# First mixer: tile 1 for TensorE's convolution is projected ahead of k, v and q and convolved between the first scores; one projected unit stands between attention blocks

## The chip, the cores and the metric

The kernel runs on one core of a Trainium2 chip. The metric is the device time of one execution in microseconds (us): the median of three runs. The engines are called PE (TensorE), DVE (VectorE), ACT (ScalarE), POOL (GpSimd) and SP (SyncE, which issues DMA transfers). L160 is line 160 of the kernel.

## The reference

One inference step of a two-layer decoder: 512 prompt tokens and 8 x 8 sample tokens, 576 columns in all, width 1024, float32. Layer 0 mixes with a gated causal convolution (width 31) beside windowed attention, layer 1 with a Mamba-2 scan; a convolutional feed-forward block follows each. Only the mixer of layer 0 is touched:

```python
def even_mixer(h, conv_hist, k_hist, v_hist, start, w_in, conv_w, conv_b, ln_g, ln_b, qn_g, kn_g, sinks, w_out):
    a_val, a_gate, q, k, v = jnp.split(
        h @ w_in, [CONV_A_DIM, 2 * CONV_A_DIM, 2 * CONV_A_DIM + qd, 2 * CONV_A_DIM + qd + kd], axis=-1)
    u = a_val * jax.nn.sigmoid(a_gate)
    padded = jnp.concatenate([conv_hist, u], axis=1)
    c = jax.nn.silu(layernorm(causal_dwconv(padded, conv_w, conv_b), ln_g, ln_b))
    new_conv = padded[:, -(CONV_A_WIDTH - 1):]
    q = partial_rope(rmsnorm(q.reshape(b, t, N_Q_HEADS, HEAD_DIM), qn_g), pos)
    k = partial_rope(rmsnorm(k.reshape(b, t, N_KV_HEADS, HEAD_DIM), kn_g), pos)
    ...
    out = jnp.concatenate([c, o], axis=-1) @ w_out
    return out, new_conv, k_all[:, -WINDOW:], v_all[:, -WINDOW:]
```

CONV_A_DIM is 512, so the convolution has four tiles of 128 channels. The attention has 8 query heads of 64 on 2 key heads, a window of 128, and a learned sink per head; the prompt is done in four blocks of 128 queries, which see 128 keys (block 0) or 256.

## The kernel before

Channels lie on the 128 partitions, the 576 tokens along them, in two halves of 288. A **unit** (`units`) projects 128 output channels: one weight tile of 128 x 1024 comes by DMA on SP's queue (L141, three buffers `wr`), is split into a high part on ACT (L150) and a low part on DVE (L151), and each half takes 24 matmuls, three for each of eight input tiles (`mm3`, L160 to L162), into a PSUM bank of the ring "mm". Behind each half its closure evacuates the bank: `a_gate(i)` scales and applies the sigmoid, `a_val(i)` writes the gated values of convolution tile i into `cap[i]` and `cas`, and others serve k, v and q (norm sums, rotary product L461, transposes of v). The first mixer has 14 units: gate(i) and val(i) for i = 0 to 3, k, v, q0 to q3.

Tiles 0 and 2 are convolved on DVE with 31 taps each (L434, L436). The taps are handed out a few at a time behind the halves of units (`then_taps`) or alone (`some_taps`). Tiles 1 and 3 (`PC`) are convolved on TensorE by `pe_conv(i)`: the closure of val(i) stores the tile to a scratch in DRAM, `cad[i]` (L415, L416); `pe_conv` builds the weights `w4` on POOL (L544), reads the tile back with 32 transfers on SP's queue, 16 into `xp4` and 16 into `xs4`, each shifted by a column (L555, L556), and then runs 32 matmuls with 32 output columns over the 512 prompt tokens (L563), 32 over the samples (L570), and two evacuations (L574, L575). It is a generator: the first `next` issues weights and transfers, the rest comes when it is taken up again.

Attention per block n: `scores(n)` does eight matmuls (L629) and the softmax, which is DVE's maximum (L601), ACT's exponential (L608), DVE's sums and reciprocals (L609, L610) and POOL's normalisation, one product per head (L612). `values(n)` transposes the probabilities in chunks of 128 keys (L644, TensorE), has ACT copy them out of PSUM (`ptb`, L646), multiplies by v (`po`, L649) and has ACT copy the result (`of`, L657). `sample_loads`, `sample_scores` and `sample_values` do the same for the sample tokens against cached keys. After them the output projection runs over the attention tiles (`oh`), then the layer norm over the four convolved tiles (mean matmul `pm`, L756), then the output projection over these (`cc`).

PSUM has eight banks in rings by purpose; from the first scores on they are mm = [0, 1], aux = [4 to 7], sc = [4, 5, 6], pt = [7, 2], po = [3]. The order of the instructions on each engine is fixed when the program is built: a scheduler takes the program's order as a priority and moves an instruction ahead where another isn't ready, so units, scores and convolution interleave. Each engine then runs its list in that order.

Of the kernel before, what the change touches and what calls it, by code (L numbers as in the profile page):

```python
# [50 lines left out]
class Builder:  # L51
# [300 lines left out]
    def mix0(self):  # L352
# [15 lines left out]
        cos, sin = self.S("cos"), self.S("sin")  # L368
# [21 lines left out]
        PC, NPTB = (1, 3), 3  # L390
# [49 lines left out]
        def some_taps(n):  # L440
            for _ in range(n):
                next(taps, None)

        def then_taps(unit, n):
            src_, m, evac = unit

            def go(half, p):
                evac(half, p)
                some_taps(n)
            return src_, m, go  # L450
# [82 lines left out]
        nc.sync.dma_start(sin, d["sin"])  # L533
        nc.vector.tensor_scalar(pq, self.cv("prot", 0, P), self.pv("q_g"), None, op0=MUL)
        nc.vector.tensor_scalar(pk, self.cv("prot", 0, P), self.pv("k_g"), None, op0=MUL)
        self.units([then_taps(u, n) for u, n in zip(qkv, (1, 2, 1, 1, 1, 1))], 1)
        self.free(kg, ksq, krs, vf, cos, sin)

        self.rings = {"mm": [0, 1], "aux": [4, 5, 6, 7], "sc": [4, 5, 6], "pt": [7, 2], "po": [3]}

        def pe_conv(i):
            w4 = [self.S("w4", NP) for _ in range(2)]
            for a in range(2):
                nc.gpsimd.tensor_tensor(w4[a].rearrange("p (k m) -> p k m", m=32),  # L544
                                        self.cv("m32", 0, 32).unsqueeze(1).broadcast_to([P, 16, 32]),
                                        self.pv("ca_wq", i * 32 + a * 16, 16).unsqueeze(2).broadcast_to([P, 16, 32]), op=MUL)
            xp4 = [self.S("xp4", 540) for _ in range(4)]
            xsp = [self.S("xs4", 608) for _ in range(2)]
            xs4 = [xsp[c // 2][:, (c % 2) * 304:(c % 2) * 304 + 304] for c in range(4)]
            src = cad[i]  # L550
            for c in range(4):
                for j in range(4):
                    n = 540 if j < 3 else 536
                    r, rc = slice(j * 32, j * 32 + 32), slice(c * 32, c * 32 + 32)
                    nc.sync.dma_start(xp4[c][r, 0:n], src[rc, j:j + n])  # L555
                    nc.sync.dma_start(xs4[c][r, 0:304 - j], src[rc, 542 + j:846])  # L556
            yield
            pp, ps = self.pm(), self.pm()
            for s in range(8):
                k = slice(0, P if s < 7 else 96)  # L560
                for c in (3, 2, 1, 0):
                    w = w4[s // 4][k, (s % 4 * 4 + c) * 32:(s % 4 * 4 + c) * 32 + 32]
                    m = nc.tensor.matmul(pp[c * 32:c * 32 + 32, :], w, xp4[c][k, 4 * s:4 * s + NP], start=s == 0, stop=s == 7)  # L563
                    if s or c < 3:
                        self.tc.keep_in_program_order(m)
            for s in range(8):
                k = slice(0, P if s < 7 else 96)
                for c in range(4):
                    w = w4[s // 4][k, (s % 4 * 4 + c) * 32:(s % 4 * 4 + c) * 32 + 32]
                    m = nc.tensor.matmul(bt(ps[c * 32:c * 32 + 32, 0:64]), w, xs4[c].rearrange("p (b t) -> p b t", t=38)[k, :, 4 * s:4 * s + 8],  # L570
                                         start=s == 0, stop=s == 7)
                    self.tc.keep_in_program_order(m)
            ca[i] = self.S("ca")
            nc.vector.tensor_scalar(ca[i][:, :NP], pp, self.pv("ca_b", i), None, op0=ADD)  # L574
            nc.vector.tensor_scalar(ca[i][:, NP:], ps[:, 0:64], self.pv("ca_b", i), None, op0=ADD)  # L575
            self.free(xp4, xsp, w4)
            yield


        rq = self.ps("rq")  # L580
        for bh in range(2):
# [36 lines left out]
        def scores(n):  # L618

            k0 = max(n - 1, 0) * P  # L620
            width = (n + 1) * P - k0
            sc = [None] * 8
            for j in range(4):
                if j % 2 == 0:
                    p = [self.ps("sc", "sc") for _ in range(2)]
                for kv in range(2):
                    rows = slice(kv * 64, kv * 64 + 64)
                    o = sc[kv * 4 + j] = p[kv][:, (j % 2) * width:(j % 2 + 1) * width]
                    nc.tensor.matmul(o, qf[j][rows, n * P:(n + 1) * P], kf[rows, k0:k0 + width], start=True, stop=True)  # L629
            return softmax(sc, self.cv("amask", 256 - width, width), rsq[:, n * 8:n * 8 + 8],  # L630
                           self.pv("sink_p", 0, 8), nsink[:, 0:8], width, (0, 1, 4, 5, 2, 3, 6, 7))

        def values(n, probs):

            pr, held = probs
            po = self.ps("po", "po")
            k0 = max(n - 1, 0)
            nch = n + 1 - k0
            for c in range(nch):
                ptb = []  # L640
                for kv in range(2):
                    pt = self.ps("pt", "pt")
                    for j in range(4):
                        nc.tensor.transpose(pt[:, j * P:(j + 1) * P], pr[kv * 4 + j][:, c * P:(c + 1) * P], self.ident)  # L644
                    ptb.append(self.Z("ptb", NP, bufs=NPTB))
                    nc.scalar.activation(ptb[-1], pt, AF.Copy)  # L646
                ch = k0 + c
                for kv in (1, 0):
                    m = nc.tensor.matmul(po[kv * 64:kv * 64 + 64, :], vt[:, ch * P + kv * 64:ch * P + kv * 64 + 64], ptb[kv],  # L649
                                         start=c == 0, stop=c == nch - 1)  # L650
                    if kv == 0:
                        self.tc.keep_in_program_order(m)
            self.free(held)
            if not of:
                of.extend(self.S("of") for _ in range(4))
            for j in range(4):
                nc.scalar.activation(of[j][:, n * P:(n + 1) * P], po[:, j * P:(j + 1) * P], AF.Copy)  # L657
# [4 lines left out]
        def sample_loads():  # L662
            for i in range(2):
                kct.append(self.S("kct", 512))
                vc.append(self.S("vc", 512))
                nc.sync.dma_start(kct[i], d["kct"][i])
                nc.sync.dma_start(vc[i], d["vc"][i])
                nc.sync.dma_start(d["wk_old"][i], kct[i].rearrange("p (b s) -> p b s", s=P)[:, :, 8:])
                nc.sync.dma_start(d["wv_old"][i], vc[i][8:, :])
# [3 lines left out]
        def sample_scores():  # L673
            for bh in range(2):
                p = [self.ps("sc", "sc") for _ in range(2)]
                for b4 in range(4):
                    b = bh * 4 + b4
                    for kv in range(2):
                        rows = slice(kv * 64, kv * 64 + 64)
                        nc.tensor.matmul(p[kv][b4 * 32:b4 * 32 + 32, 0:P], qs[rows, b * 32:b * 32 + 32],  # L680
                                         kct[bh][rows, b4 * P:(b4 + 1) * P], start=True, stop=True)
                for kv in range(2):
                    rows = slice(kv * 64, kv * 64 + 64)
                    nc.tensor.matmul(p[kv][:, P:192], qs[rows, bh * P:(bh + 1) * P], kf[rows, NP:], start=True, stop=True)
                c0 = 32 + bh * 2
                probs.append(softmax([p[kv][:, 0:192] for kv in range(2)], self.cv("smask", bh * 192, 192), rsq[:, c0:c0 + 2],
                                     self.pv("sink_s", 0, 2), nsink[:, 8:10], 192, (0, 1)))
# [25 lines left out]
                nc.scalar.activation(bt(of[j][:, NP:]), po_v[:, :, j, :], AF.Copy)  # L713

        p0 = scores(0)
        self.units([then_taps(gate_unit(2), 2)], 1)
        p1 = scores(1)
        self.units([then_taps(val_unit(2), 2), then_taps(gate_unit(1), 2)], 1)
        values(0, p0)
        p2 = scores(2)  # L720
        self.units([then_taps(val_unit(1), 2), then_taps(gate_unit(3), 2)], 1)
        values(1, p1)
        p3 = scores(3)
        self.units([then_taps(val_unit(3), 2)], 1)
        self.norm_end()
        convs = [pe_conv(i) for i in PC]
        next(convs[0])
        sample_loads()
        values(2, p2)
        sample_scores()  # L730
        some_taps(5)
        next(convs[1])
        values(3, p3)
        for _ in convs[0]:
            pass
        some_taps(5)
        sample_values()
        for _ in convs[1]:
            pass
        self.rings = {"mm": [2, 3, 0, 1], "aux": [4, 5, 6, 7]}  # L740
        oh = [self.pair("o") for _ in range(4)]
# [608 lines left out]
```

## Time and profile before

| What | us |
|---|---|
| median of three runs | 1605.51 |
| lowest and highest run | 1602.03, 1608.3 |
| profiled execution, its own time | 1610.28 |
| span of its profile | 1608.5 |
| TensorE busy in the span | 1569.8 |
| unit k begins on TensorE | 24.78 |
| last matmuls of the unit q3 end | 73.30 |
| output projection begins | 178.16 |
| convolution of tile 3 begins | 188.17 |

The span is what the profiler saw of one execution; its time is measured around it and is 1.8 us longer. The mean granted clock of TensorE was 0.988 of full speed. Times in the trace count from the span's start. The whole change lies between 24.78 and about 200 us, an eighth of the span; the rest is the other layer and the feed-forward blocks. A row of the timeline gives start, length, engine, line, what is written from what, and in brackets the idle time ahead with what ended it. A group's row gives count, busy time, mean of one in ns, and idle time ahead.

### The profile page before, as it was taken

How to read it: one execution, taken by the hardware profiler on the slowest of the kernel's cores; microseconds unless marked ns; L12 is line 12 of the kernel's file. 1: busy time of each engine (PE TensorE's matmuls, PEld its weight loads, DVE VectorE, ACT ScalarE, POOL GpSimd, SP SyncE). 2: the span in 40 equal slices, each digit the busy share in tenths (PEclk: the TensorE clock that was granted, in tenths of full speed). 3: DMA queues.
4: the chain of work that ended last, by engine and by line, in shares of the span. 5: the costliest groups of instructions: out<-in, count | busy, mean ns of one | idle time of the engine just before them, and what ended most of it. 6: DMA issues, size and time to landing. Idle time of an engine off the chain costs nothing.

```text
span 1608.5 us, 28729 instructions
## 1 busy us (share of the span) xinstructions
PE 1569.8 (98%) x11709; PEld 1484.2 (92%) x11709; DVE 999.5 (62%) x1750; ACT 660.6 (41%) x1213; POOL 150.5 (9%) x362
## 2 busy tenths in 40 slices
PE   8997999999999999999999999999999999999999
PEld 7985699999999999998988998898799999999999
DVE  7877386664455355668786676676776653564552
ACT  6265263222222123479665546556453221221220
POOL 0045001000000000011201101111101000000000
PEclk9998999999999999999999999999999999999999
DMA  7116222222222222226235226236322222222222
GB/s 228 58 57 141 70 79 91 92 79 79 90 81 73 93 83 78 74 82 178 101 87 186 99 74 193 80 104 175 106 80 87 84 80 86 86 71 89 91 82 75
DMA packets 69841, 157.60 MB, mean 98 GB/s; under 512 B 20158, under 2 KB 24510, under 8 KB 69710
## 3 DMA queue, kind: packets, MB, share of 16 engines
q1 hardware_dynamic: 69710, 155.77, 31.4%
q8 instruction: 92, 1.51, 0.4%
q14 instruction: 39, 0.32, 0.1%
HBM read 140.54 MB, written 15.21 MB: 97 GB/s over the span
## 4 chain that ended last, share of the span: by engine, by line
PE 85%; DVE 6%; ACT 4%; DMA 3%; issue 1%; POOL 1%; SPq 0%; ACTq 0%; DVEq 0%
PE mm L160 25%; PE mm L162 25%; PE mm L161 25%; DMA acb<-acd 2%; DMA h<-in_h 1%; PE yp L1045 1%; PE pyo L1062 1%; DVE cconv L799 1%; PE mm L563 1%; PE pt L182 1%; DVE ca L436 1%; PE pst L988 1%; POOL sm L612 1%; ACT wh L150 1%; PE pr L193 1%
## 5 line engine op out<-in xcount | busy, mean ns | idle before, releaser
L160 PE MATMUL mm<-hh,wh 128*128 128x288 f32 (+1 forms) x2288 | 685.0, 300 | 8.8 <-ACT wh L150 8.1
L162 PE MATMUL mm<-hh,wl 128*128 128x288 f32 x2288 | 680.1, 298 | 0.0
L161 PE MATMUL mm<-hl,wh 128*128 128x288 f32 (+1 forms) x2288 | 679.5, 297 | 0.0
L150 ACT ACTIVATE wh<-wr 128x1024 fp32r<-128x1024 f32 (+1 forms) x215 | 223.2, 1039 | 543.6 <-issue 275.5
L160 PEld LDWEIGHTS mm<-hh,wh 128*128 128x128 f32 (+1 forms) x2288 | 431.4, 189 | 15.2 <-ACT wh L150 8.3
L161 PEld LDWEIGHTS mm<-hl,wh 128*128 128x128 f32 (+1 forms) x2288 | 432.1, 189 | 6.3 <-issue 4.7
L162 PEld LDWEIGHTS mm<-hh,wl 128*128 128x128 f32 x2288 | 431.8, 189 | 2.5 <-issue 1.1
L151 DVE TENSOR_TENSOR wl<-wr,wh 128x1024 fp32r<-128x1024 f32 (+1 forms) x215 | 258.4, 1202 | 76.9 <-ACT wh L150 76.6
L160 PE MATMUL mm<-yh,wh 128*128 128x288 f32 x960 | 286.1, 299 | 2.3 <-ACT yh L170 2.2
L161 PE MATMUL mm<-yl,wh 128*128 128x288 f32 x960 | 287.6, 300 | 0.1
L162 PE MATMUL mm<-yh,wl 128*128 128x288 f32 x960 | 284.9, 298 | 1.3 <-DVE wl L151 1.3
L162 PEld LDWEIGHTS mm<-yh,wl 128*128 128x128 f32 x960 | 181.2, 189 | 6.0 <-issue 4.1
L161 PEld LDWEIGHTS mm<-yl,wh 128*128 128x128 f32 x960 | 181.3, 189 | 5.2 <-issue 4.0
L160 PEld LDWEIGHTS mm<-yh,wh 128*128 128x128 f32 x960 | 181.1, 189 | 4.7 <-ACT yh L170 2.6
L259 DVE TENSOR_TENSOR x<-x,mm 128x288 f32<-128x288 f32 x192 | 85.4, 450 | 157.3 <-PE mm L162 157.2
L304 DVE TENSOR_TENSOR gbuf<-mm,rs 128x224 f32<-128x224 f32 x44 | 17.2, 392 | 108.1 <-PE mm L162 108.1
L315 ACT ACTIVATE gsilu<-gconv,par 128x512 f32<-128x512 f32 x44 | 31.8, 724 | 115.3 <-DVE gconv L312 115.3
L312 DVE SCALAR_TENSOR_TENSOR gconv<-gbuf,par,gconv 128x592 f32<-128x592 f32 x88 | 73.1, 831 | 1.5
L325 DVE TENSOR_TENSOR gsilu<-mm,gsilu 128x288 f32<-128x288 f32 x88 | 40.0, 454 | 49.8 <-PE mm L162 49.8
L799 DVE SCALAR_TENSOR_TENSOR cconv<-cbuf,par,cconv 128x600 f32<-128x600 f32 x72 | 61.5, 858 | 13.0 <-ACT cconv L797 12.0
L307 POOL COPY fpo<-gbuf 128x2 f32<-128x2 f32 x44 | 11.3, 258 | 499.3 <-DVE gbuf L304 499.3
L1070 POOL TENSOR_TENSOR h<-h,cds 128x512 f32<-128x512 f32 x32 | 36.6, 1163 | 189.4 <-PE pyo L1062 132.7
(307 smaller groups left out, 1653.8 us busy)
## 6 DMA issues: line engine op xcount, KB each, us to landing
wr<-in_w_gate SPq DMA_DIRECT2D x44, 512.0 KB, 3.3
wr<-in_w_up SPq DMA_DIRECT2D x44, 512.0 KB, 3.3
wr<-in_w_in_o SPq DMA_DIRECT2D x40, 512.0 KB, 3.5
wr<-in_w_down SPq DMA_DIRECT2D x32, 448.0 KB, 3.3
wr<-in_w_down SPq DMA_DIRECT2D x16, 512.0 KB, 3.5
acb<-acd SPq DMA_DIRECT2D x32, 256.0 KB, 4.0
h<-in_h SPq DMA_DIRECT2D x32, 256.0 KB, 3.7
out_ssm_s<-h SPq DMA_DIRECT2D x32, 256.0 KB, 2.1
```

Of the source, the lines that this page charges most:

```text
L150: nc.scalar.activation(hi[:, :n], raw[:, :n], AF.Copy)
L151: nc.vector.tensor_tensor(lo[:, :n], raw[:, :n], hi[:, :n].bitcast(F32), op=SUB)
L160: nc.tensor.matmul(out, hi[:, ws], xh[:, sl], start=i == 0, stop=False)
L161: nc.tensor.matmul(out, hi[:, ws], xl[:, sl], start=False, stop=False)
L162: nc.tensor.matmul(out, lo[:, ws], xh[:, sl], start=False, stop=i == n - 1)
L259: nc.vector.tensor_tensor(self.x[m][:, sl], self.x[m][:, sl], p[:, :HB], op=ADD)
L304: nc.vector.tensor_tensor(g[:, 290:514], p[:, 0:224], rs[:, HB:NP], op=MUL)
L312: nc.vector.scalar_tensor_tensor(cv[:, :592], g[:, k:592 + k], w(k), cv[:, :592], op0=MUL, op1=ADD)
L315: nc.scalar.activation(sl[:, :NP], cv[:, :NP], AF.Silu, bias=b)
L325: nc.vector.tensor_tensor(sl[:, HALF[half]], p[:, :HB], sl[:, HALF[half]], op=MUL)
L799: nc.vector.scalar_tensor_tensor(cv[:, :600], g[:, k:600 + k], w(k), cv[:, :600], op0=MUL, op1=ADD)
L1070: nc.gpsimd.tensor_tensor(hp(h0[b4]), hp(h0[b4]), cds[:, b * 32 + 8 * g:b * 32 + 8 * g + 8].unsqueeze(2).broadcast_to([P, 8, 64]), op=MUL)
```

## The change

gate(1) and val(1) are projected ahead of k. The transfers of tile 1's convolution are issued after q1, ahead of q2 and q3, and its matmuls stand between scores(0) and scores(1). gate(2), val(2) and gate(3) stand one by one between the blocks of attention, and val(3) after values(2); sample_loads comes ahead of val(3), and sample_scores ahead of tile 3's transfers. The rings are set after q3 as before. No instruction is added or removed. Lines of the moved region count four higher in the changed kernel (scores L633, transposes L648, copies L650, po L653, exponentials L612), the convolution's count four lower (L559, L566; transfers L551, L552).

```diff
@@ mix0: units of k, v and q @@
-        self.units([then_taps(u, n) for u, n in zip(qkv, (1, 2, 1, 1, 1, 1))], 1)
-        self.free(kg, ksq, krs, vf, cos, sin)
-
-        self.rings = {"mm": [0, 1], "aux": [4, 5, 6, 7], "sc": [4, 5, 6], "pt": [7, 2], "po": [3]}
 
         def pe_conv(i):
...
+        qkv = [then_taps(u, n) for u, n in zip(qkv, (1, 2, 1, 1, 1, 1))]
+        self.units([then_taps(gate_unit(1), 2), then_taps(val_unit(1), 2)], 1)
+        self.units(qkv[:4], 1)
+        convs = {i: pe_conv(i) for i in PC}
+        next(convs[1])
+        self.units(qkv[4:], 1)
+        self.free(kg, ksq, krs, vf, cos, sin)
+        self.rings = {"mm": [0, 1], "aux": [4, 5, 6, 7], "sc": [4, 5, 6], "pt": [7, 2], "po": [3]}
...
         p0 = scores(0)
+        for _ in convs[1]:
+            pass
+        p1 = scores(1)
         self.units([then_taps(gate_unit(2), 2)], 1)
-        p1 = scores(1)
-        self.units([then_taps(val_unit(2), 2), then_taps(gate_unit(1), 2)], 1)
         values(0, p0)
         p2 = scores(2)
-        self.units([then_taps(val_unit(1), 2), then_taps(gate_unit(3), 2)], 1)
+        self.units([then_taps(val_unit(2), 2)], 1)
         values(1, p1)
         p3 = scores(3)
+        self.units([then_taps(gate_unit(3), 2)], 1)
+        values(2, p2)
+        sample_loads()
         self.units([then_taps(val_unit(3), 2)], 1)
         self.norm_end()
-        convs = [pe_conv(i) for i in PC]
-        next(convs[0])
-        sample_loads()
-        values(2, p2)
         sample_scores()
+        next(convs[3])
         some_taps(5)
-        next(convs[1])
         values(3, p3)
-        for _ in convs[0]:
-            pass
         some_taps(5)
         sample_values()
-        for _ in convs[1]:
+        for _ in convs[3]:
             pass
```

How the scheduler sets this shows at three places. The first is TensorE between the last unit of q3 and the second scores; `mm_913` is the bank of gate(2), `sc` are scores, `rq` small sums for the norms of q. Before:

```order
L461 MATMUL pr_841<-qg_797,pq_205 128x288
L629 MATMUL sc_863<-kf_213,qf_210 128x128
L487 MATMUL rq_829<-cst_110,qsq_826 128x2 x4
L160 MATMUL mm_913<-hh_115,wh_909 128x288
L582 MATMUL rq_847<-cst_110,qss_212 128x2 x2
L161 MATMUL mm_913<-hl_116,wh_909 128x288
L162 MATMUL mm_913<-hh_115,wl_910 128x288
L160 MATMUL mm_913<-hh_117,wh_909 128x288
L629 MATMUL sc_858<-kf_213,qf_208 128x128
```

In the changed kernel `mm_1086` is the bank of tile 1's convolution:

```order
L559 MATMUL mm_1086<-xp4_826,w4_822 32x512
L461 MATMUL pr_1020<-qg_976,pq_205 128x288
L487 MATMUL rq_1008<-cst_110,qsq_1005 128x2 x4
L586 MATMUL rq_1026<-cst_110,qss_212 128x2 x2
L633 MATMUL sc_1042<-kf_213,qf_210 128x128
L559 MATMUL mm_1086<-xp4_829,w4_822 32x512
L559 MATMUL mm_1086<-xp4_828,w4_822 32x512
L559 MATMUL mm_1086<-xp4_827,w4_822 32x512
L559 MATMUL mm_1086<-xp4_826,w4_822 32x512
L633 MATMUL sc_1037<-kf_213,qf_208 128x128
```

The matmuls between the small sums and the first scores are the convolution's, not those of gate(2).

The second place is ACT behind the last projected unit. Before, all copies of the probabilities (`ptb`) stand ahead of the sample scores' exponentials (`sm_1639`, `sm_1668`, and `es` for the sinks):

```order
L646 ACTIVATE ptb_1750<-pt_1745 128x512
L646 ACTIVATE ptb_1757<-pt_1752 128x512
L657 ACTIVATE of_1183<-po_1728 128x128
L657 ACTIVATE of_1184<-po_1728 128x128
L657 ACTIVATE of_1185<-po_1728 128x128
L657 ACTIVATE of_1186<-po_1728 128x128
L608 ACTIVATE sm_1639,den_1636<-sm_1639,neg_1637,rsq_207 128x192
L606 ACTIVATE es_1638<-es_1638 128x2
```

In the changed kernel `ptb_1803` and `ptb_1810` are the first two copies of values(3):

```order
L650 ACTIVATE ptb_1803<-pt_1798 128x512
L612 ACT_TABLE_LOAD
L612 ACTIVATE sm_1708,den_1705<-sm_1708,neg_1706,rsq_207 128x192
L610 ACTIVATE es_1707<-es_1707 128x2
L612 ACTIVATE sm_1708,den_1705<-sm_1708,neg_1706,rsq_207 128x192
L612 ACTIVATE sm_1737,den_1734<-sm_1737,neg_1735,rsq_207 128x192
L610 ACTIVATE es_1736<-es_1736 128x2
L612 ACTIVATE sm_1737,den_1734<-sm_1737,neg_1735,rsq_207 128x192
L650 ACTIVATE ptb_1810<-pt_1805 128x512
```

The sample exponentials and a table load stand between two copies of values(3), for which TensorE's `po_1797<-ptb_1810` is the next reader. On TensorE, behind the transposes into `pt_1805`, the changed kernel has:

```order
L648 MATMUL pt_1805<-ident_73,sm_1475 128x128 x2
L758 MATMUL pm_1992<-ca_335,o512_101 128x288
L648 MATMUL pt_1814<-ident_73,sm_1472 128x128 x2
L648 MATMUL pt_1814<-ident_73,sm_1473 128x128 x2
L758 MATMUL pm_1992<-ca_1152,o512_101 128x288
L653 MATMUL po_1797<-ptb_1810,vt_218 64x512
```

Four transposes and two matmuls of the mean stand between the transposes and the product that needs their copy.

The third place is SP's queue. Before, tile 1's stores and transfers follow val(1) late, among the weights of the output projection:

```order
L415 DMA cad1_203<-cap_1128 128x542
L416 DMA cad1_203<-cas_201 128x304
L555 DMA xp4_1536<-cad1_203 32x540 x3
L555 DMA xp4_1536<-cad1_203 32x536
L141 DMA wr_2278<-in_w_out_e 128x1024
```

In the changed kernel they stand among the weights of q (`wr_945` is q3's):

```order
L415 DMA cad1_203<-cap_376 128x542
L416 DMA cad1_203<-cas_201 128x304
L141 DMA wr_945<-in_w_in_e 128x1024
L551 DMA xp4_826<-cad1_203 32x540 x3
L551 DMA xp4_826<-cad1_203 32x536
```

The last of them is followed by the weights of gate(2), `wr_1205`:

```order
L551 DMA xp4_829<-cad1_203 32x540
L552 DMA xs4_831<-cad1_203 32x303
L551 DMA xp4_829<-cad1_203 32x540
L552 DMA xs4_831<-cad1_203 32x302
L551 DMA xp4_829<-cad1_203 32x536
L552 DMA xs4_831<-cad1_203 32x301
L141 DMA wr_1205<-in_w_in_e 128x1024
```

All 32 transfers of tile 1 have moved between the weights of two projected units, with the stores of k and v among them.

## The prediction

> **What bounds the kernel now.** The page's first part and its chain come first: which engine is busy for the whole span, and whose work ended last.
>
> ```profile
> span 1608.5 us, 28729 instructions
> PE 1569.8 (98%) x11709; PEld 1484.2 (92%) x11709; DVE 999.5 (62%) x1750; ACT 660.6 (41%) x1213; POOL 150.5 (9%) x362
> PE 85%; DVE 6%; ACT 4%; DMA 3%; issue 1%; POOL 1%; SPq 0%; ACTq 0%; DVEq 0%
> ```
>
> TensorE is busy for 98% of the span and holds 85% of the chain, so time is won only where TensorE stands still or where its clock is cut. The change adds and removes no work; it moves it inside the first mixer. So the next view is the busy time by window over the stretch that the change rearranges, from the end of q3 to the second tile that is convolved on TensorE.
>
> ```profile
> core 0: us, PE busy (x) PEld busy (x) DVE busy (x) ACT busy (x) POOL busy (x), PEclk, DMA share, GB/s
> 44.00:74.00 30.00, 30.00 (x217) 28.95 (x217) 26.54 (x47) 5.98 (x11) 0.12 (x1) 1.00 0.22 73
> 78.00:88.00 10.00, 10.00 (x36) 8.55 (x37) 5.00 (x25) 1.87 (x3) 0.00 (x0) 0.50 0.15 45
> 88.00:139.00 51.00, 49.31 (x342) 42.88 (x342) 44.97 (x114) 38.29 (x92) 29.73 (x29) 1.00 0.33 79
> 139.00:143.00 4.00, 1.71 (x15) 1.23 (x15) 3.93 (x6) 4.00 (x13) 1.42 (x1) 0.96 0.19 40
> 143.00:145.00 2.00, 2.00 (x6) 0.39 (x6) 1.93 (x5) 1.12 (x2) 0.00 (x0) 0.50 1.25 158
> 145.00:149.00 4.00, 1.29 (x5) 0.70 (x5) 3.96 (x6) 0.60 (x1) 3.11 (x2) 0.86 0.82 127
> 149.00:163.00 14.00, 11.43 (x35) 3.71 (x35) 2.24 (x3) 3.96 (x12) 5.80 (x7) 0.52 0.70 197
> 163.00:178.00 15.00, 14.97 (x223) 7.98 (x220) 4.52 (x22) 5.75 (x21) 3.00 (x4) 0.99 0.53 130
> 188.00:197.00 9.00, 9.00 (x135) 3.70 (x134) 1.58 (x4) 0.00 (x0) 0.00 (x0) 1.00 0.01 2
> ```
>
> A loss in a window is its idle time plus busy time times the missing part of the clock. At the first scores (78 to 88) TensorE never idles but has a granted clock of 0.50: 10.00 x 0.50 = 5.0 us lost. From 88 to 139 it idles 51.00 - 49.31 = 1.7 us. From 139 to 163 it idles 24.00 - (1.71 + 2.00 + 1.29 + 11.43) = 7.6 us, and the clock takes 1.71 x 0.04 + 2.00 x 0.50 + 1.29 x 0.14 + 11.43 x 0.48 = 6.7 us more. From 163 on nothing is lost. The total is **21.0 us**, and the rearranged stretch can win no more than that. From 163 on TensorE has no gap, so what is won before then moves everything behind it.
>
> What does it wait for? The waits and the timeline of TensorE say.
>
> ```profile
> PE pt L644 <- POOL sm L612: 4.5, 5, 2.4
> PE pt L644 <- ACT ptb L646: 2.9, 2, 2.3
> PE sc L629 <- DVE mx L601: 1.0, 1, 1.0
> ...
> 24.78 0.29 PE L160 MATMUL mm<-hh,wh 128*128 128x288 f32 x1
> 73.30 0.65 PE L461 MATMUL pr<-qg,pq 128*128 128x288 f32 x2
> 75.17 1.05 PE L487 MATMUL rq<-cst,qsq 128*128 128x2 f32 x8
> 130.38 1.08 PE L649 MATMUL po<-ptb,vt 128*64 128x512 f32 x4
> 132.45 0.40 PE L160 MATMUL mm<-hh,wh 128*128 128x288 f32 x1
> 138.94 1.03 PE L644 MATMUL pt<-ident,sm 128*128 128x128 f32 x8
> 142.27 0.74 PE L644 MATMUL pt<-ident,sm 128*128 128x128 f32 x4 [2.29 <-ACT ptb L646]
> 148.36 0.33 PE L644 MATMUL pt<-ident,sm 128*128 128x128 f32 x1 [2.40 <-POOL sm L612]
> 188.17 2.35 PE L563 MATMUL mm<-xp,w 128*32 128x512 f32 x20
> 196.12 0.75 PE L756 MATMUL pm<-ca,o 128*128 128x288 f32 x2
> ```
>
> The last projected unit ends at 138.94. Behind it stand the transposes of values(2) and values(3) with no projection between them, and they wait for ACT's copies out of PSUM and for POOL's normalisation of scores(3). That is the place to fill.
>
> **The change part by part.** The price of one unit is 138.94 - 132.45 = 6.5 us of TensorE, or 6.4 where no score stands in it.
>
> The units gate(1) and val(1) go ahead of k. They cost 2 x 6.4 = 12.8 us there and are gone by as much between the blocks, so they are free in themselves. What could spoil them is VectorE, 26.54 of 30.00 us busy (88%) in the q stretch. The two units bring their own evacuations and eight taps of the vector convolution; before, the same instructions stood between the blocks, where VectorE is 44.97 of 51.00 us busy, the same 88%. I cost them at 0; the cover is the 12% that is free, and without it each late evacuation would hold a PSUM bank for one of the 0.8 us taps.
>
> The convolution of tile 1 needs its 32 reloads from DRAM, which are now issued on SP ahead of the weights of gate(2).
>
> ```profile
> 121.62 0.44 SPq L416 DMA_DIRECT2D cad<-cas  x1
> 127.15 1.72 SPq L555 DMA_DIRECT2D xp<-cad  x4
> 143.12 0.44 SPq L416 DMA_DIRECT2D cad<-cas  x1
> 157.50 0.40 SPq L555 DMA_DIRECT2D xp<-cad  x1
> 166.38 1.46 SPq L555 DMA_DIRECT2D xp<-cad  x1
> 174.07 0.42 SPq L556 DMA_DIRECT2D xs<-cad  x1
> ...
> cad<-cap SPq DMA_DIRECT2D x2, 271.0 KB, 6.2
> xp<-cad SPq DMA_DIRECT2D x24, 67.5 KB, 2.0
> ```
>
> From store issue to first reload is 127.15 - 121.62 = 5.5 us. The 32 reloads of tile 3 ran at (174.07 - 157.50) / 31 = 0.53 us apart and landed 2.0 us later. In the changed kernel val(1) ends at 24.78 + 12.8 = 37.6, the store leaves near 40, the reloads could start near 46, and the last of them reuses a slot that the third q-side unit frees: k, v and q0 end at 37.6 + 3 x 6.4 = 56.8, and q0's rotary work stands behind that, so about 65. At the worst all 32 follow from there: 65 + 17 + 2 = 84. TensorE arrives at 73.30 + 12.8 = 86.1. So nothing waits; if the order lets part of them go earlier, the slack is some 12 us. The weights of gate(2), queued behind on SP, so go out at 82 at the latest, and gate(2) comes after two score blocks and the convolution, past 95. The two POOL products for the convolution's weights stand in an empty POOL (0.12 us busy from 44 to 74).
>
> Between scores(0) and the rest now stands the convolution (196.12 - 188.17 = 7.9 us) where gate(2) stood. Both fill TensorE while VectorE and ACT work on the scores. The question is the clock of 0.50. It starts behind the small matmuls at 75.17 with no idle time in front. They stay, now between 32-column convolution matmuls, and those ran at a clock of 1.00 from 188 on. So the bounds are 0 and 5.0 us lost. I take 0, since the row of the convolution itself is full clock, and keep 5.0 as a case. [...]
>
> Between the blocks there is now one unit per gap, with two left over for the end: gate(3) beside values(1), val(3) beside values(2). Each such pair has 6.4 us of matmuls with which to cover the ACT copies and POOL.
>
> ```profile
> L612 POOL TENSOR_SCALAR sm<-sm,den 128x256 f32<-128x256 f32 x24 | 27.2, 1151 | 6.3 <-DVE den L610 6.3
> L646 ACT ACTIVATE ptb<-pt 128x512 f32<-128x512 f32 x14 | 7.9, 589 | 11.9 <-PE pt L644 11.9
> L608 ACT ACTIVATE sm<-sm,neg,rsq 128x192 f32<-128x192 f32 x4 | 2.2, 541 | 3.7 <-DVE neg L604 3.7
> L608 ACT ACTIVATION_READ_ACCUMULATOR sm<-sm,neg,rsq 128x1 f32 x36 | 6.7, 186 | 0.0
> L608 ACT ACT_TABLE_LOAD x2 | 2.6, 1283 | 0.0
> 165.98 0.19 ACT L606 ACTIVATE es<-es 128x2 f32<-128x2 f32 x1
> ```
>
> The sample loads, eight transfers that stood ahead of tile 3's reloads on SP, now stand ahead of val(3) and are not waited for.
>
> POOL needs 8 x 1.15 = 9.2 us per block. Scores(3) now has gate(3) and the rest of values(1), values(2) and val(3) behind it, over 20 us, before values(3) wants it: POOL's 4.5 us of waits go. Of the waits for ACT's copies two small ones are left, estimated at 1.0 us (values(1) with gate(3)) and 0.6 us (values(2) with val(3)), from the copies' 0.59 us each; bounds 0 and the 2.3 us that the longest took. The 1.0 us wait of the score matmuls is the other part of the 1.7 and goes, since the convolution now stands there.
>
> A new wait comes at the end. On ACT the second copy of values(3) now stands behind the sample scores' softmax: one table load, four exponentials, their four accumulator reads, two small exponentials. That is 1.28 + 4 x 0.54 + 4 x 0.19 + 2 x 0.19 = 4.6 us, and 0.6 for the copy itself; TensorE has four transposes (half of the 1.03 us row) and two matmuls of the mean (the 0.75 us row) beside it, some 1.2 us. So it idles 4.6 + 0.6 - 1.2 = **4.0 us**; behind the waiting matmul the other transposes, the sample values and the output projection queue up. The bounds are 0 and 5.0 (a gap of 1.0 us for VectorE's maxima more). Afterwards the clock: rows at half clock show 2.00 us at 0.50 (1.0 lost) and the first scores 10.00 us at 0.50 (5.0 lost). I take the middle, 3.0 us.
>
> The sum: before loses 21.0, the changed kernel 1.0 + 0.6 + 4.0 + 3.0 = 8.6. **Gain 12.4 us.** The convolution of tile 3 would start at 188.17 - 12.4 = 175.8.
>
> Its reloads must be there by then. val(3) still ends behind the same scores and units, but the convolution (7.9) and values(2) (16 transposes 2.1 and two groups of po 2.2, by 138.94 and 130.38) now stand ahead of it too: 138.94 + 7.9 + 4.3 + 1.6 of small waits - 5.0 - 1.7 = 146.0. Before the change the second store was issued 143.12 - 138.94 = 4.2 us behind that end, and 5.5 us later the reloads could go: 155.7. The 32nd follows 31 x 0.53 = 16.4 us behind, and lands at 174.1. So under 2 us are left; this is the thinnest cover of the change, and without the cut of 3.0 TensorE would be there 1.3 us before the tile.
>
> The profiled execution took 1610.28 us, 1.8 beyond its span, against a median of 1605.51 (1602.03 to 1608.3), 4.8 above it. Against its own time the sum gives 1610.3 - 12.4 = 1597.9. I take half of the 4.8 as that execution's own, 2.4, so 1595.5.
>
> **The rivals.** First, both cuts: the first scores run at half clock as they do now. Gain 12.4 - 5.0 = 7.4, so 1600.5. For it speaks that the small matmuls are still there and that no idle time was needed. Second, no cut at all: gain 15.4 less the 1.3 us for which it would then wait for the tile, 14.1, so 1593.8; for it speaks that the new idle gap is single and the work behind it dense. Third, the waits at the transposes only change place: all that 139 to 163 loses now (7.6 + 6.7 = 14.3) comes back where values(3), the taps and the sample softmax meet, and only the front wins 6.7: 1601.2. For it speaks VectorE, full from 139 to 149 (3.93 + 1.93 + 3.96 of 10 us), from which the sample maxima must come.
>
> Fourth, the other side: the reload of tile 3 becomes what TensorE waits for. One mechanism: 32 transfers issued one by one on SP from 155.7 on. The gain is gone when the last lands at 188.2, that is at (188.2 - 2.0 - 155.7) / 31 = 0.98 us apart; slower by over 0.5% needs 196.2, or 1.24 us. The slowest issue of before took 1.46 us, the mean was 0.53 at a DMA share of 0.53 to 0.70. At 1.4 us the start is 155.7 + 43.4 + 2.0 = 201.1, 12.9 late: 1620.8. Fifth, the change doesn't do what it says: tile 1's reloads are late and the convolution stalls the first scores instead of filling them. By the above it needs the reloads 2 to 12 us later than worked out; 6 us of stall leave 1601.5.
>
> **How the numbers follow.** About 0.5%, 8 us, is what a measurement of this kernel can tell from no change: faster is under 1597.5, slower over 1613.5. Chances: the forecast 0.42 (1592 to 1599), both cuts 0.24 (1600.5), no cut 0.16 (1594), waits that change place 0.09 (1601), the late reload 0.05 (1621), tile 1 late 0.04 (1601). Faster takes 0.38 of the forecast, all of no cut and 0.05 of both cuts: 0.59. Slower is the fourth rival: 0.05. The rest, 0.36, is within. The range reaches up past the both-cuts and change-of-place cases to 1604, and down to a kernel without the 4.0 us gap and the cut, whose reloads start some 4 us earlier than worked out because no tap holds up val(3)'s evacuation: gain 19.4, so 1588.
>
> **What would show it.** Right: a clock of 1.00 over the first scores with convolution matmuls between them; no wait of a transpose for POOL; one idle gap of about 4 us late in values(3), put down to ACT's copies; convolution of tile 3 starting near 176 without a wait for a DMA. Wrong: a clock of 0.50 near 90, gaps at gate(3), a TensorE wait for the reloaded tile, or work behind the mixer that differs from before by more than a us.

## The result, and the profile after

The changed kernel takes 1595.84 us, the median of four runs (1593.19 to 1596.65), against 1606.9 before (1602.03 to 1608.64): a ratio of 0.9933, with a 95% interval of 0.9907 to 0.996. The prediction was 1595.5, in a range of 1588 to 1604. In a second series of six runs the ratio was 0.9935 (0.9921 to 0.9949).

The page of the changed kernel has the same bound as before:

```profile
span 1594.9 us, 28738 instructions
PE 1560.2 (98%) x11709; PEld 1479.2 (93%) x11709; DVE 999.7 (63%) x1750; ACT 656.1 (41%) x1210; POOL 149.4 (9%) x362
```

Busy TensorE time fell by 9.6 us with the same 11709 matmul records, for the most part by the clock (granted at 0.988 of full speed on average before, at 0.996 now); the other 4.0 of the 13.6 us of span are idle time. The profile shows one difference in the work: ACT loads its tables 49 times, 52 before. The windows of the changed kernel, cut at the events of interest (the columns are those of the windows before):

```profile
86.99:101.90 14.91, 14.91 (x159) 6.89 (x158) 7.37 (x31) 6.84 (x22) 0.00 (x0) 1.00 0.11 37
101.90:150.46 48.56, 47.46 (x346) 38.34 (x342) 36.59 (x108) 33.94 (x86) 33.65 (x34) 1.00 0.29 79
152.60:155.90 3.30, 0.25 (x2) 0.00 (x0) 3.30 (x9) 3.29 (x13) 0.20 (x1) 1.00 0.66 77
156.68:160.10 3.42, 3.42 (x14) 1.78 (x12) 3.28 (x5) 1.24 (x3) 2.96 (x4) 0.50 0.41 91
160.10:176.07 15.97, 15.16 (x126) 12.86 (x124) 8.07 (x13) 4.15 (x14) 0.00 (x0) 1.00 0.53 135
```

From 86.99 to 101.90 stand scores(0) and tile 1's convolution, at a granted clock of 1.00 where 0.50 was shown before. Then TensorE idles 48.56 - 47.46 = 1.1 us up to 150.46, 3.1 us in one gap before 155.90, and 0.8 us before the output projection; one stretch of 3.42 us at half clock costs 1.7 us. That is 6.7 us lost against 21.0 before. Its waits and the start of tile 3's convolution:

```profile
PE po L653 <- ACT ptb L650: 3.6, 2, 3.1
PE mm L160 <- ACT oh L170: 0.6, 1, 0.6
PE sc L684 <- DVE mx L605: 0.5, 1, 0.5
PE mm L161 <- DVE ol L171: 0.3, 1, 0.3
...
176.07 2.35 PE L559 MATMUL mm<-xp,w 128*32 128x512 f32 x20
```

The transposes no longer wait for POOL at all; the long wait left is that of a product for ACT's copy. Tile 3's convolution starts at 176.07, 12.1 us earlier than the 188.17 of before. The other 1.5 of the 13.6 us lie behind the mixer. The prediction calls over 1 us there a sign of being wrong, but the sign can't tell: that stretch took 1420.3 and 1416.7 us in two profiles of the kernel before.

### The profile page after: what moved, and what is told of

It reads as the page before. It is cut to its first block, busy times and chain, and to the rows that moved or that the text cites. A ratio compares the mean times of both kernels' runs of the same rounds, so it can differ in the third digit from the quotient of the medians.

```text
span 1594.9 us, 28738 instructions
## 1 busy us (share of the span) xinstructions
PE 1560.2 (98%) x11709; PEld 1479.2 (93%) x11709; DVE 999.7 (63%) x1750; ACT 656.1 (41%) x1210; POOL 149.4 (9%) x362
## 4 chain that ended last, share of the span: by engine, by line
PE 82%; DVE 7%; ACT 4%; DMA 4%; issue 1%; POOL 1%; SPq 0%; ACTq 0%; DVEq 0%; POOLq 0%
PE mm L160 24%; PE mm L161 24%; PE mm L162 24%; DMA acb<-acd 2%; DVE cconv L801 1%; PE mm L559 1%; PE yp L1047 1%; DMA h<-in_h 1%; PE pyo L1064 1%; PE pt L182 1%; DVE ca L436 1%; ACT wh L150 1%; DVE wl L151 1%; ACT acb L1021 1%; PE pr L193 1%
```

## Experiments

A cut is a stretch in which the granted clock is 0.50. Where an experiment's own start of tile 3 is given, it is its first matmul on `xp` behind 170 us, beside 188.17 (before) and 176.07 (changed). It is a sharper measure than the total, since the stretch behind it took between 1416.7 and 1423.1 us in the thirteen profiles. Still each is one execution: two profiles of the changed kernel lie 0.7 us apart (176.07, 176.75), two of the kernel with gate(2) put back 3.2 (173.74, 176.95).

**The kernel before, again.**

> The kernel before, unchanged. Theory: the granted clock of 0.50 at the first scores belongs to what TensorE does there, so a second profile shows it again from about 78 us for some 10 us, and the convolution of tile 3 begins near 188 us. Rival: the cut falls by chance, and a second profile has a clock of 1.00 there; tile 3 then begins near 183 us, and 5 us of the change's gain were luck of one profile.

Measured: 1606.29 us; tile 3 at 187.83; a clock of 0.50 again from 77.9 to 88.1. The cut is there in both profiles of this kernel.

**gate(2) put back between the first scores.**

```diff
         p0 = scores(0)
+        self.units([then_taps(gate_unit(2), 2)], 1)
+        p1 = scores(1)
         for _ in convs[1]:
             pass
-        p1 = scores(1)
-        self.units([then_taps(gate_unit(2), 2)], 1)
         values(0, p0)
```

> The changed kernel with gate(2) back between scores(0) and scores(1), and the convolution of tile 1 behind scores(1). Theory: the convolution's matmuls among the small ones keep the clock; with gate(2) there the clock is 0.50 for some 10 us again, 5 us are lost, some 2 us are won back because the convolution now runs in whole groups of four, and tile 3 begins near 179 us (176.1 in the changed kernel), total about 1599 us. Rival: the two units ahead of k, which move all this by 13 us, are what takes the cut away; then the clock stays at 1.00 and tile 3 begins near 174 us, total about 1594 us.

Measured: 1596.84 us (0.9923, 0.9904 to 0.9942); tile 3 at 173.74; no clock cut at the first scores (1.00 from 84 to 108.58). So the theory failed, and what the rival forecast came: the convolution isn't needed there to keep the clock. That the two units alone keep it, as the rival said, is tried below with only these two moved, and fails. And values(0) came earlier. The convolution and the first transposes behind it, in this kernel's timeline of TensorE:

```profile
100.68 7.08 PE L559 MATMUL mm<-xp,w 128*32 128x512 f32 x64
107.57 1.08 PE L566 MATMUL mm<-xs,w 128*32 128x64 f32 x64
108.58 0.66 PE L648 MATMUL pt<-ident,sm 128*128 128x128 f32 x4
```

All 32 matmuls of the convolution over the prompt (two records each) take 107.57 - 100.68 = 6.9 us here. In the changed kernel they stand among the scores:

```profile
90.31 1.06 PE L559 MATMUL mm<-xp,w 128*32 128x512 f32 x8
91.31 0.71 PE L633 MATMUL sc<-kf,qf 64*128 64x128 f32 x4
91.95 1.06 PE L559 MATMUL mm<-xp,w 128*32 128x512 f32 x6
92.94 0.71 PE L633 MATMUL sc<-kf,qf 64*128 64x128 f32 x4
93.58 1.04 PE L559 MATMUL mm<-xp,w 128*32 128x512 f32 x2
94.55 0.49 PE L633 MATMUL sc<-kf,qf 64*128 64x128 f32 x2
94.97 1.06 PE L559 MATMUL mm<-xp,w 128*32 128x512 f32 x6
```

A whole group of four columns (eight records) holds TensorE for 91.31 - 90.31 = 1.0 us, one column alone (two records) for 94.55 - 93.58 = 0.97: the four run side by side, and a group that a score splits is paid twice. Two of the eight groups were split (from 91.95 and from 94.97), 1.9 us. At its end this version has a new wait in place of the copy's:

```profile
PE pt L698 <- POOL sm L616: 3.7, 2, 3.1
```

These are the transposes of the sample tokens.

**Sample scores last.**

```diff
-        sample_scores()
         next(convs[3])
         some_taps(5)
         values(3, p3)
+        sample_scores()
         some_taps(5)
         sample_values()
```

> The changed kernel with the sample scores behind values(3), so that ACT copies all of values(3) before the sample exponentials. Theory: the 3.05 us wait of po for its copy goes, with the half clock behind it (1.7 us), but only some 2 us can be won, since tile 3's reloads land near 174 us: tile 3 begins at 174 us and waits there for its transfers; total about 1594 us. Rival: the wait moves on, because the sample softmax now ends later and the sample values and the output projection wait for it: tile 3 begins at 176 us or later, total 1596 us or more.

Measured: 1602.67 us (0.9966, 0.9945 to 0.9986); tile 3 at 180.99. The rival held, and more: the sample transposes now wait for POOL, and the clock is halved for 13.65 us behind it.

```profile
PE pt L698 <- POOL sm L616: 4.6, 2, 4.2
...
158.00:172.00 14.00, 11.23 (x64) 7.98 (x65) 7.48 (x13) 4.55 (x14) 3.91 (x4) 0.51 0.49 111
```

So the 3.1 us wait of the changed kernel seems to buy something: its exponentials for the sample stand early.

**The convolution ahead of scores(0).**

```diff
-        p0 = scores(0)
         for _ in convs[1]:
             pass
+        p0 = scores(0)
         p1 = scores(1)
```

> The changed kernel with tile 1's convolution ahead of scores(0) in the program, so that its groups of four matmuls aren't broken up by scores. Theory: a group that is split into three and one takes 2 x 0.97 us instead of 0.97, two groups are split now, so scores(1) ends 1.9 us earlier, and tile 3 begins near 174.2 us; total about 1594 us. Rival: the scores come later, and values(0) waits for POOL's normalisation, 6.8 us for block 0: the gain is given back ahead of values(0), tile 3 begins near 176 us.

Measured: 1598.8 us (0.9939, 0.992 to 0.9957); tile 3 at 178.47. The groups are whole, but the scores come late, and values(0) runs into POOL's products for block 0. Its waits and windows:

```profile
PE pt L648 <- POOL sm L616: 1.3, 5, 0.3
...
101.00:112.00 11.00, 9.61 (x65) 7.92 (x63) 3.54 (x17) 10.97 (x36) 4.68 (x8) 1.00 0.00 0
112.00:119.00 7.00, 7.00 (x26) 5.10 (x24) 5.65 (x24) 2.74 (x6) 4.71 (x4) 0.52 0.00 0
```

The waits up to 112 us cost 1.4 us, and right behind them the clock is halved for 6.8 us, 3.4 lost. The 1.9 us are more than given back, as the rival said, but for the larger part by the clock, which it didn't name.

**Only the two units ahead of k.**

```diff
+        self.units([then_taps(gate_unit(1), 2), then_taps(val_unit(1), 2)], 1)
         self.units([then_taps(u, n) for u, n in zip(qkv, (1, 2, 1, 1, 1, 1))], 1)
...
-        self.units([then_taps(val_unit(2), 2), then_taps(gate_unit(1), 2)], 1)
+        self.units([then_taps(val_unit(2), 2)], 1)
...
-        self.units([then_taps(val_unit(1), 2), then_taps(gate_unit(3), 2)], 1)
+        self.units([then_taps(gate_unit(3), 2)], 1)
```

> The kernel before with only gate(1) and val(1) moved ahead of k; tile 1 is still reloaded and convolved behind val(3), and gate(2), val(2), gate(3), val(3) stand where they stood. Theory: moving the two units in itself takes away the cut of the clock at the first scores (as with gate(2) put back there) and nothing else, since values(2) and values(3) still have no unit beside them: tile 3 begins near 183 us (188.2 before), with 13 to 15 us still lost around the last values; total about 1601 us. Rival: the cut belongs to the kernel without the convolution at the front; clock 0.50 at the first scores, tile 3 near 188 us, total about 1606 us.

Measured: 1603.2 us (0.9975, 0.9956 to 0.9993); tile 3 at 182.58. The place fits the theory, its reason doesn't: the clock at the first scores is still cut, to 0.50 for 10.24 us, and the gain lies in the tail.

```profile
91.26:101.50 10.24, 10.24 (x40) 9.27 (x41) 4.75 (x24) 3.25 (x7) 0.00 (x0) 0.50 0.16 54
139.00:163.00 24.00, 18.68 (x122) 7.46 (x119) 17.74 (x32) 9.48 (x28) 10.19 (x11) 0.79 0.64 140
...
PE pt L645 <- POOL sm L613: 4.6, 5, 2.1
PE pt L645 <- ACT ptb L647: 0.3, 1, 0.3
```

TensorE idles 24.00 - 18.68 = 5.3 us there (7.6 before). The clock takes 18.68 x 0.21 = 3.9 us there (6.7 before). The waits for POOL are about the 4.5 us of before, those for ACT fell from 2.9 to 0.3. Two of the ten runs took 1596.3 and 1596.8 us, at a mean granted clock of 0.996 and 0.994; the other eight took 1602.1 to 1604.6, at 0.990 to 0.994. A second profile of the same kernel:

> The kernel before with only gate(1) and val(1) ahead of k, once more. Its ten times lay at 1602 to 1605 eight times and at 1596 to 1597 twice. Theory: the profile, if the execution is of the lower group, has a clock of 1.00 at the first scores; if of the upper, 0.50 for some 10 us. Rival: the profile shows 0.50 there whatever its time.

Measured: 1603.31 us, of the upper group; the cut from 91.3 to 101.5 again, tile 3 at 182.48. No profile shows an execution of the lower group, so whether it lacks the cut stays open.

**The units early, as before.**

```diff
+        self.units([then_taps(gate_unit(2), 2)], 1)
         p1 = scores(1)
-        self.units([then_taps(gate_unit(2), 2)], 1)
+        self.units([then_taps(val_unit(2), 2)], 1)
         values(0, p0)
         p2 = scores(2)
-        self.units([then_taps(val_unit(2), 2)], 1)
+        self.units([then_taps(gate_unit(3), 2)], 1)
         values(1, p1)
         p3 = scores(3)
-        self.units([then_taps(gate_unit(3), 2)], 1)
-        values(2, p2)
-        sample_loads()
         self.units([then_taps(val_unit(3), 2)], 1)
         self.norm_end()
+        sample_loads()
+        values(2, p2)
         sample_scores()
```

> The changed kernel with the units placed early as before: gate(2) and the convolution ahead of scores(1), val(2) ahead of values(0), gate(3) ahead of values(1), val(3) ahead of values(2), nothing between values(2) and values(3). Theory: the spread units are what hides the copies and POOL; without them TensorE idles 5 to 8 us around values(2) and values(3), with a clock of 0.50 behind it: tile 3 begins near 183 us (176.1 in the changed kernel), total about 1602 us. Rival: the early units only exchange one wait for another and tile 3 begins within 2 us of 176.

Measured: 1599.48 us (0.9965, 0.995 to 0.9981); tile 3 at 178.40. Waits for POOL are back, but small:

```profile
PE pt L648 <- POOL sm L616: 2.6, 4, 0.7
PE sc L684 <- DVE mx L605: 0.9, 1, 0.9
...
139.00:163.00 24.00, 20.08 (x135) 12.07 (x134) 20.71 (x45) 14.57 (x44) 17.04 (x16) 0.93 0.47 103
```

TensorE idles 3.9 us from 139 to 163 and has one cut of 3.42 us. In these two profiles spreading the units is worth 178.4 - 176.1 = 2.3 us, less than half of the least that the theory expected, and just over the rival's bound. By itself that is within what two profiles of one kernel can differ; the medians (1599.48 here, 1595.84 and 1596.99 for the changed kernel) point the same way.

**Tile 3 reloaded twice.**

```diff
-            for c in range(4):
+            for c in (0, 1, 2, 3) * (2 if i == 3 else 1):
                 for j in range(4):
```

> The changed kernel with tile 3's 32 reloads issued twice, the same data into the same place. Theory: the last reload now lands 2 us ahead of TensorE's need, so of some 15 us more of issue 12 to 13 show: tile 3 begins near 188.5 us and waits there for a DMA. Rival: the reload has more cover than that, and tile 3 begins less than 10 us later than 176.1.

Measured: 1607.8 us; tile 3 at 186.62, 10.6 later.

```profile
PE mm L559 <- DMA xp<-cad: 10.0, 1, 10.0
```

The wait is there, and it is a DMA's. It is 10 us, not the 12 to 13 of the theory: the first reload went out at 154.90 instead of 156.56, so this profile had some 1.7 us more cover.

**Sample scores early.**

```diff
+        sample_loads()
         self.units([then_taps(gate_unit(3), 2)], 1)
         values(2, p2)
-        sample_loads()
+        sample_scores()
         self.units([then_taps(val_unit(3), 2)], 1)
         self.norm_end()
-        sample_scores()
         next(convs[3])
```

> The changed kernel with the sample loads ahead of gate(3) and the sample scores ahead of val(3), so that the sample exponentials lie beside a unit. Theory: the 3.05 us wait for the copy behind the exponentials goes, the half clock behind it (1.7 us) too, and VectorE's sample maxima no longer stand between the last taps; tile 3 would begin near 171.5 us but its reloads land near 174 us, so it begins at 174 us: total about 1594 us. Rival: as with the sample scores placed last, another wait takes its place (values(3) for POOL), and tile 3 begins at 176 us or later.

Measured: 1597.34 us (0.9943, 0.9923 to 0.9962); tile 3 at 179.49. The wait for the copy behind the exponentials is gone, and the fourth rival of the prediction stands in its place:

```profile
PE mm L559 <- DMA xp<-cad: 3.8, 1, 3.8
...
88.66:92.07 3.41, 3.41 (x30) 2.31 (x31) 2.50 (x7) 1.61 (x2) 0.00 (x0) 1.00 0.45 151
92.07:98.89 6.82, 6.82 (x21) 1.93 (x20) 1.53 (x13) 0.00 (x0) 0.00 (x0) 0.50 0.02 5
```

val(3) ends later than in the changed kernel, its first reload goes out at 162.47 (156.56 there), and TensorE waits 3.8 us for the tile. This profile also has 6.82 us of half clock at the first scores, 3.4 us lost, though up to there TensorE's order is that of the changed kernel. It took 1604.41 us, 7.1 more than the median, so how long the wait is in most executions is not shown.

**The changed kernel, and the one with gate(2) put back, again.**

> The changed kernel once more, nothing changed, with more timings. Theory: the cut of the clock at the first scores comes and goes between executions of one program; then its times fall into two groups some 3 to 7 us apart, or the profile has a clock of 0.50 near 92 us that the first one had not. Rival: the cut belongs to the order of the instructions; then times lie within some 4 us and the profile shows 1.00 again, and what the version with early sample scores showed near 92 us has another reason.

> The version with gate(2) between scores(0) and scores(1) and tile 1's convolution in whole groups behind scores(1), once more, on the chip and in the rounds of the changed kernel. Theory: whole groups win some 2 us ahead of values(0), of which the wait of the sample transposes for POOL gives half back: 1 to 2 us below the changed kernel, within the noise. Rival: it beats the changed kernel by over 3 us.

Measured: 1596.99 us (six runs, 1592.48 to 1598.54; 0.9935, 0.9921 to 0.9949) and 1596.28 us (1593.58 to 1600.71; 0.9937, 0.9922 to 0.9952). The first has no cut at the first scores (1.00 from 85.99 to 100.90), two of 3.42 us later (1.7 us each), and tile 3 at 176.75. Neither theory nor rival fits whole: there is no cut at the first scores, yet the times spread over 6.1 us, and the fastest run had a mean granted clock of 0.999, the slowest three 0.993 to 0.994. The second has again no cut at the first scores (1.00 from 78 to 154), but one of 10.24 us from 157.65, behind 2.1 us of idle time from 154.23 on, and tile 3 at 176.95, so the 2 us that it won are gone in that execution. No version that was run beats the changed kernel by more than the measurement can tell.

## Why the prediction was right, step by step

**The two units ahead of k cost nothing there: right.** q3's first rotary product, right behind the unit's last matmuls, begins at 86.41, 13.1 us behind the 73.30 of before, where two units make 12.8.

**Tile 1's reloads are hidden: right.** First and last of the 32, on SP:

```profile
47.29 3.93 SPq L551 DMA_DIRECT2D xp<-cad  x6
...
70.14 0.42 SPq L552 DMA_DIRECT2D xs<-cad  x1
```

The first was forecast near 46, the last to have landed by 84 at the worst; TensorE's first convolution matmul came at 86.99 and waited for nothing.

**The first scores at full clock: right in outcome, not in its reason.** I took 0 because the convolution itself had been seen at full clock. With gate(2) in its place there was no cut either, in two profiles; with gate(2) and without the convolution at the front there was, in four; and with the convolution there was one in one profile of seven. The section on the hardware has what the profiles show of it; what decides stays open.

**The waits at the transposes go: right, with a better cause to be told.** Of the 4.5 us for POOL and 2.9 for ACT before nothing is left at the transposes; the smaller of the two waits in the 3.6 us row, 0.5 us, is a product's (0.7 before). But spread units are only part of it: the two units at the front moved tile 3 by 5.6 us (182.58), the convolution between the scores by 4.2 more (178.40), in which the cut's absence is contained, and the spread units by 2.3 (176.07). These are differences of single profiles, and the second step also takes tile 1's transfers out of the tail. I had put all that goes from 139 to 163 down to the spread.

**The new gap: right in place and cause, too large.** Forecast 4.0, measured 3.05 us. ACT in the changed kernel:

```profile
151.66 1.28 ACT L612 ACT_TABLE_LOAD   x1
152.95 0.55 ACT L612 ACTIVATE sm<-sm,neg,rsq 128x192 f32<-128x192 f32 x1
153.40 0.19 ACT L612 ACTIVATION_READ_ACCUMULATOR sm<-sm,neg,rsq 128x1 f32 x1
...
155.28 1.05 ACT L650 ACTIVATE ptb<-pt 128x512 f32<-128x512 f32 x2
```

From the table load to the copy are 155.28 - 151.66 = 3.6 us, where the sum had 4.6: I had added up durations, but they overlap: the exponential of 0.55 us at 152.95 is followed 0.45 us later by its accumulator read.

**The cut behind it: 3.0 forecast as a middle of 1.0 and 5.0, 1.7 measured,** and 3.4 in the second profile.

**The sum.** Lost were 6.7 us instead of 8.6. By that alone tile 3 would have begun 21.0 - 6.7 = 14.3 us earlier; it began 12.1 earlier. The split groups are 1.9 of the difference, and q3's end 0.3. So two terms were too large by 0.95 and 1.3 us, the two small waits (1.6 forecast) were replaced by 1.9 of other ones, and a cost that the forecast lacked, the splitting of the convolution's groups by the scores, made up for them: that tile 3 was forecast at 175.8 and came at 176.07 is in good part luck. The lines of the order ahead of the prediction show one group whole (`xp4_829` to `xp4_826`); the split groups come behind them. I had counted the convolution at its 7.9 us wherever it stands.

**Tile 3's reloads: right.** Forecast were a first issue at 155.7 and under 2 us left. It went out at 156.56, the last at 171.83; 2.0 us for its landing (the medians in the changed kernel are 1.9 and 2.0) leave 2.2 us ahead of 176.07. The first and the last:

```profile
156.56 0.32 SPq L551 DMA_DIRECT2D xp<-cad  x1
...
171.83 0.42 SPq L552 DMA_DIRECT2D xs<-cad  x1
```

The kernel with doubled reloads and the one with early sample scores both ran into it.

**The execution's own share** (half of 4.8 us): the median of before came out at 1606.9 with the added run, and 1610.28 - 1606.9 = 3.4 of it was that execution's, where 2.4 were taken. The changed kernel's profiled execution was itself 0.8 above its median (1596.65, 1595.84), and 1.5 us were won behind the mixer, which the sum had at nothing; so the nearness of 1595.5 to 1595.84 is luck too.

## What to carry to other kernels

Filling a wait with work of the same engine paid only up to the next late thing: the further repairs of the tail met POOL (waits of 3.7 us with gate(2) put back, 4.6 with the sample scores last) or a reload (3.8 us with early sample scores). Matmuls that ran side by side in column groups were cheaper as whole groups: each group that a score split cost 0.97 us more, though no version here turned that into a shorter time. Where a stretch at half clock is part of the sum, the runs here speak for pricing it in whole steps of 3.4 us and leaving the number of steps to the range, since it varied between executions of one program: one such step between 102 and 176 us in the first profile of the changed kernel, two in the second.

## What the runs showed of the hardware

Every stretch at half clock from 70 to 210 us in the thirteen profiles is a multiple of one length: 3.42 us (changed kernel, 156.68), 6.82 (early sample scores), 10.24 (before, and only the two units ahead), 13.65 (sample scores last). Windows of the kernel before, set to that length:

```profile
74.42:77.84 3.42, 3.42 (x24) 2.72 (x22) 2.27 (x8) 1.50 (x5) 0.00 (x0) 1.00 0.00 0
77.84:88.08 10.24, 10.24 (x38) 8.74 (x37) 5.24 (x25) 2.11 (x3) 0.00 (x0) 0.50 0.15 46
88.08:91.49 3.41, 3.41 (x27) 3.12 (x26) 2.64 (x6) 3.40 (x14) 0.00 (x0) 1.00 0.04 17
```

In the eleven profiles that show more than one such stretch there, they start whole steps of that length apart: in the kernel before at 77.84, 142.70 and 149.54, which are 19.0 and 2.0 steps apart; with early sample scores at 92.06 and 180.80, 26.0 steps. By the granted clock each step costs 1.7 us where TensorE is busy. The matmuls of 128x288 in the kernel before start 0.24 us apart at 0.50 (from 81.24) and 0.13 at 1.00 (from 88.30), which makes some 1.5 us a step.

The cut at the first scores came without idle time ahead of it: from 74.42 to 88.08 TensorE is 100% busy. The small matmuls for q's norms (128x2, 1.6 us in all, from 75.17) stand ahead of the cut. Where the steps lay at these matmuls is an estimate, counted back in whole steps from the cuts of each profile. By it they lay wholly inside one step in the four profiles with gate(2) at the first scores that show the cut (before twice, only the two units twice; in the first of them 75.17 to 76.81 inside 74.42 to 77.84), and the cut began at the end of that step; they lay across two steps in the two profiles that don't (gate(2) put back, twice), in the second of them by only 0.1 of their 1.5 us. With the convolution's matmuls around them they lay inside one step in six of seven profiles, and one of the six had a cut (early sample scores, where the first of them starts within 0.02 us of the step's start). That the alignment decides is therefore a guess from thirteen profiles: no run varied it alone, and it doesn't tell the five that kept the clock from the one that lost it. What took the cut away, 5.0 of the 12.1 us, stays open: the two units alone did not (two profiles), and the convolution was not needed (two others).
